# Recording the modulation's steps by the vector engine's spare time, and the norms' reciprocal roots in PSUM, in a two-block transformer kernel

## The chip, the cores and the metric

The kernel runs on one core of one Trainium2 chip. The metric is device microseconds (us) of one execution; a kernel's time is the median of its runs. The engines are named as in the profile: PE (TensorE, matrix multiplication), PEld (its weight loads), DVE (VectorE), ACT (ScalarE), POOL (GpSimd) and SP (SyncE, which issues the DMAs here).

## The reference, cut to what matters

Two stacks follow each other on one sequence of 512 tokens of width 1024. Each has two layers. All of it is float32.

```python
def first_block(x, c, w_mod, b_mod, ...):
    c_act = silu(c)
    for l in range(2):
        mod = (c_act @ w_mod[l] + b_mod[l]).reshape(1, 9, 1024)
        h = rmsnorm(x, g) * (1 + mod[:, 1]) + mod[:, 0]
        x = x + 0.5 * mod[:, 2] * swiglu(h, ...)
        h = rmsnorm(x, g) * (1 + mod[:, 4]) + mod[:, 3]
        x = x + mod[:, 5] * hybrid_mixer(h, ...)     # windowed attention, linear recurrence, short convolution
        h = rmsnorm(x, g) * (1 + mod[:, 7]) + mod[:, 6]
        x = x + 0.5 * mod[:, 8] * swiglu(h, ...)
    return rmsnorm(x, g_final)

def second_block(x, c, ctx, c_ctx, ...):             # 256 context tokens run beside the 512
    for i in range(2):
        m, mc = six vectors of silu(c) @ ada_w[i] + ada_b[i], and of c_ctx
        y, yc = mla_mixer(...) if i == 0 else na_mixer(...)
        h = layer_norm(ALPHA * h + g1 * y)
        h = layer_norm(ALPHA * h + g2 * conv_ffn(h * (1 + sc2) + sh2))
        # in layer 0 the same for the context
```

The modulation is the matrix-vector products `c_act @ w_mod` and `silu(c) @ ada_w`: 30 chunks of 1024 outputs that need only `c`, not `x`.

## The kernel before

Every activation stands transposed: eight tiles of 128 features by 512 tokens. A float32 operand is split into a rounded high part and a low part (`wh`, `wl` for weights, `hh`, `hl` and others for activations), and each product is three matmuls (`mm3`). So PE does three passes; ACT makes the high parts, DVE subtracts to get the low parts (`wl<-wr,wh`), and SP streams the weights, 256 KB a DMA.

The program is not issued as it is written. A `Recorder` collects all operations, `schedule` simulates them with a table of costs, and `emit` issues them in the order that this gave, one fixed queue for each engine. An operation's rank is its place in the recording. So where a step is *recorded* decides where the planner tries to place it, and each engine then runs its queue in order: an operation that isn't ready holds all behind it. The profile shows nearly every instruction at line 444, the issuing line in `emit`, so it is read by tile names.

`Core.run` draws the recording from three generators. `main` is the large chain. `side` is the context stream (tiles `hc`, `a`, matmuls `ps<-a,wh` of 256 columns), which gets a share of PE's recorded time and can't begin before the context's modulation of layer 0 is there (`ctx_stream` yields "wait" until then). The third is `gen_mods`, the modulation. One of its steps is one block of 128 outputs: two DMAs of 256 KB (`mr<-in_wmod`, `mr<-in_wada`), and for each a product with `silu(c)` with a row sum. Two of three products are one DVE instruction (`mr,c<-mr,b_c`, or `mj,c<-mr,b_c`); every third is a POOL product (`mr<-mr,b_c`) and an ACT sum. A step of `ada_w` that serves the context too has twice the products. DVE does 400 of these instructions in all, POOL 208. In the kernel before, `run` records one step for each 6150 ns of recorded PE time of `main`, evenly, whatever DVE has to do there; `mod` records the missing steps at once where a modulation is needed.

The stages by the trace, in us: start and first FFN of layer 0 to 405, its mixer to 605, second FFN to 1005, layer 1 the same (mixer 1430 to 1620) to 2095, latent attention to 2440, convolution FFN to 2860, neighbourhood attention to 3245, convolution FFN to the end.

A norm goes in three moves. `colsum` squares and adds the tiles and sums over features by matmuls with a column of ones (`ps<-ones,acc`) into a PSUM bank, one column for each 128 tokens. `rsqrt` makes the reciprocal root on DVE from an integer seed and three Newton steps of three instructions, on tiles of 128x2 or 128x4, each needing the one before. `bcast` transposes the result across the partitions (`ps<-ident,c`). There are 27 such roots: 3 over 512 tokens, 24 over 256. The norm of a stage is made by halves of 256 tokens (`rms_part`, `final_part`, `ln_part`), so that one half's norm can lie beside the other half's matmuls. In `ln_part` (layer norms) three of the eight subtractions `x<-x,bm` are DVE's and five are POOL's.

The planner knows that DVE and POOL hinder each other: `schedule` marks POOL's operations, and those of DVE that read and write no PSUM (`o.port`), and lets them wait for each other.

Of the kernel before, what the change touches and what calls it, by code (L numbers as in the profile page):

```python
# [16 lines left out]
ALU = mybir.AluOpType  # L17
AX = mybir.AxisListType

P = 128  # L20
D = 1024
KD = D // P
S = 512
C = 256
# [3 lines left out]
ALPHA = (2.0 * DEPTH) ** 0.25  # L28
# [32 lines left out]
LAGS = 2  # L61
FIRST = (100, 16)
HEAVY = 0.5
FIRST_POOL = (1, 3)
ON_DVE, ON_DVE_LAST = 1, 1
BEGIN = 20000.0
# [380 lines left out]
class Lag:  # L447
# [14 lines left out]
    def next(self):  # L462
        steps = self.q.pop(0)()
        if steps is not None:
            yield from steps
        yield


class Core:
# [171 lines left out]
    def first_mods(self):  # L641
# [3 lines left out]
        for m in range(8):  # L645
            nc.later = FIRST[0] + FIRST[1] * m
            dots = []
            for ch in range(2):
                d = [self.col(1), self.col(1)]
                for h in range(2):  # L650
                    raw = self.t(s="mr")
                    nc.sync.dma_start(raw, self.io["wmod"][0, ch * 8 + m][:, h * 512:(h + 1) * 512])
                    if (2 * ch + h) % 4 in FIRST_POOL:
                        nc.gpsimd.tensor_tensor(raw, raw, self.cb["c", h], op=ALU.mult)
# [67 lines left out]
        eng.tensor_tensor(acc, sums[0], sums[1], op=ALU.add)  # L722
        return acc

    def colsum(self, tiles, T, eng=None):
        nc = self.nc
        acc = self.total(tiles, T, eng)
        st = self.ps()
        for j in range(T // P):
            nc.tensor.matmul(st[:, j:j + 1], acc[:, j * P:(j + 1) * P], self.ones, start=True, stop=True)  # L730
        return st[:, :T // P]

    def rsqrt(self, v, n):
        nc = self.nc
        y, q = self.col(n), self.col(n)
        nc.vector.tensor_scalar(y.bitcast(I32), v.bitcast(I32), -0.5, float(0x5F3759DF), op0=ALU.mult, op1=ALU.add)
        for _ in range(3):
            nc.vector.tensor_tensor(q, y, y, op=ALU.mult)
            nc.vector.scalar_tensor_tensor(q, q, -0.5, v, op0=ALU.mult, op1=ALU.mult)
            nc.vector.scalar_tensor_tensor(y, q, 1.5, y, op0=ALU.add, op1=ALU.mult)  # L740
        return y

    def bcast(self, col, T, copy=None):
# [12 lines left out]
    def rms(self, x, T, width, eps=1e-6):  # L756
        nc = self.nc
        sq = []
        for a in x:
            q = self.t(s="sq")[:, :T]  # L760
            nc.scalar.activation(q, a, AF.Square)
            sq.append(q)
        st = self.colsum(sq, T)
        v = self.col(T // P)
        nc.vector.tensor_scalar(v, st, 1.0 / width, eps, op0=ALU.mult, op1=ALU.add)
        return self.bcast(self.rsqrt(v, T // P), T)

    def modulated(self, x, bc, G, Sh, out, T):
        nc = self.nc
# [100 lines left out]
    def run(self, main, side):  # L870


        rec = self.nc
        mods, own = BEGIN, 0.0
        due = 0.0
        mark = rec.pe
        for _ in main:
            own += rec.pe - mark
            due += self.share * (rec.pe - mark)
            while mods + self.every <= own:  # L880
                mods += self.every
                next(self.modgen, None)
            while side is not None and due > 0:
                mark = rec.pe + HEAVY * rec.ve
                got = next(side, "end")
                due -= rec.pe + HEAVY * rec.ve - mark
                if got == "end":
                    side = None
                elif got == "wait":
                    due = 0.0  # L890
            mark = rec.pe

    def rms_part(self, l, sub):

# [313 lines left out]
    def ln_part(self, xs, T, l, which, kind, mod, perm=False):  # L1208

        nc = self.nc  # L1210
        n = C // P
# [5 lines left out]
        def part(sl):  # L1217
# [8 lines left out]
            sq = []  # L1226
            for a in x:
                q = self.t(s="sq")[:, :C]
                nc.scalar.activation(q, a, AF.Square)
                sq.append(q)  # L1230
            s1 = self.colsum(x, C, nc.gpsimd)
            s2 = self.colsum(sq, C)
            mu, m2, v = self.col(n), self.col(n), self.col(n)
            nc.vector.tensor_scalar(mu, s1, 1.0 / D, None, op0=ALU.mult)
            nc.vector.tensor_tensor(m2, mu, mu, op=ALU.mult)
            bm = self.bcast(mu, C, self.t(s="bm"))
            nc.vector.tensor_scalar(v, s2, 1.0 / D, 1e-5 / (ALPHA * ALPHA), op0=ALU.mult, op1=ALU.add)
            nc.vector.tensor_tensor(v, v, m2, op=ALU.subtract)
            br = self.bcast(self.rsqrt(v, n), C)
            if T == C:  # L1240
                yield
            ts = []
# [596 lines left out]
```

## Time and profile before

| | us |
|---|---|
| median of 3 runs | 3613.79 (3612.24 to 3618.5) |
| the profiled execution, whole | 3614.32 |
| its span, first to last instruction | 3612.2 |
| PE busy in the span | 3482.7 |
| DVE busy | 2697.6 |
| ACT busy | 1815.6 |
| POOL busy | 772.5 |
| DMA, mean | 132 GB/s |

The whole execution is 2.1 us longer than the span. PE is busy in nearly all of it, so what can be won are the stretches in which PE waits, and those at its lower clock. "PEclk" in a row is the granted clock as a share of the upper level of 2.4 GHz; the records show that level and half of it, 1.2 GHz.

### The profile page before, as it was taken

Reading aid. Unit: us, or ns where it says so; the run is one execution under the profiler, and the core shown is the slowest. Engines: PE = TensorE matmul, PEld = TensorE weight load, DVE = VectorE, ACT = ScalarE, POOL = GpSimd, SP = SyncE. Lnnn points to the kernel's source line nnn. Section 1 sums busy time; section 2 is a strip of 40 time slices with the busy share of each in tenths; the row PEclk is TensorE's granted clock in tenths of the full one; section 3 lists DMA queues with packets and bytes.
Section 4 is the critical chain, followed back from the end, with each engine's and each line's share of the span. In section 5 each row is a group of like instructions: output and inputs, shape, how many; then the busy total and the mean of one; then the engine's idle time right before and its main releaser. Section 6 shows DMA issues by size and latency. Waiting matters only on the chain.

```text
span 3612.2 us, 56937 instructions
## 1 busy us (share of the span) xinstructions
PE 3482.7 (96%) x19814; PEld 3055.6 (85%) x19814; DVE 2697.6 (75%) x5566; ACT 1815.6 (50%) x3932; POOL 772.5 (21%) x848
## 2 busy tenths in 40 slices
PE   6999999999999999999999999989999999989998
PEld 5888978888898889899888988879888888978887
DVE  8966899986598866976444689988667757886566
ACT  5434565564456534844333578776334444454333
POOL 4311242331023410310000034341000422330002
PEclk9999999999999999999999999999999999999999
DMA  9854355675366564534334311214333143333330
GB/s 329 293 183 149 96 156 158 196 251 156 108 213 193 157 192 139 165 101 125 111 115 135 106 49 51 63 45 138 100 104 104 55 114 107 88 97 110 97 91 24
DMA packets 276448, 475.37 MB, mean 132 GB/s; under 512 B 40000, under 2 KB 55872, under 8 KB 276160
## 3 DMA queue, kind: packets, MB, share of 16 engines
q1 hardware_dynamic: 276160, 471.74, 43.0%
q8 instruction: 156, 2.56, 0.3%
q14 instruction: 132, 1.08, 0.1%
HBM read 448.81 MB, written 5.50 MB: 126 GB/s over the span
## 4 chain that ended last, share of the span: by engine, by line
PE 82%; DVE 11%; ACT 3%; issue 2%; DMA 1%; POOL 1%; SPq 0%; DVEq 0%; POOLq 0%; ACTq 0%
PE ps L444 82%; DVE c L444 2%; DVE wl L444 1%; DVE ptl L444 1%; DVE x L444 1%; DVE pl L444 1%; DVE mr L444 1%; DVE hl L444 1%; DVE tm L444 1%; DVE acc L444 0%; ACT L444 0%; DVE os L444 0%; DVE yl L444 0%; DVE mods L444 0%; DMA mr<-in_wada 0%
## 5 line engine op out<-in xcount | busy, mean ns | idle before, releaser
L444 DVE TENSOR_TENSOR wl<-wr,wh 128x512 fp32r<-128x512 f32 (+1 forms) x1182 | 835.1, 728 | 138.0 <-ACT wh L444 116.1
L444 ACT CAST wh<-wr 128x512 fp32r<-128x512 f32 (+1 forms) x1182 | 677.5, 614 | 112.2 <-PE ps L444 75.0
L444 PE MATMUL ps<-hh,wh 128*128 128x512 f32 (+1 forms) x1864 | 689.1, 370 | 4.4 <-ACT hh L444 4.4
L444 PE MATMUL ps<-hl,wh 128*128 128x512 f32 (+1 forms) x1864 | 686.7, 368 | 6.0 <-DVE hl L444 6.0
L444 PE MATMUL ps<-hh,wl 128*128 128x512 f32 (+1 forms) x1864 | 685.7, 368 | 2.1 <-DVE wl L444 1.9
L444 PE MATMUL ps<-fh,wh 128*128 128x512 f32 (+1 forms) x1344 | 463.6, 345 | 0.0
L444 PE MATMUL ps<-fl,wh 128*128 128x512 f32 (+1 forms) x1344 | 461.9, 344 | 0.0
L444 PE MATMUL ps<-fh,wl 128*128 128x512 f32 (+1 forms) x1344 | 461.7, 344 | 0.0
L444 PEld LDWEIGHTS ps<-hl,wh 128*128 128x128 f32 x1864 | 353.6, 190 | 63.6 <-DVE hl L444 8.4
L444 PEld LDWEIGHTS ps<-hh,wh 128*128 128x128 f32 x1864 | 353.7, 190 | 61.5 <-ACT hh L444 5.6
L444 PEld LDWEIGHTS ps<-hh,wl 128*128 128x128 f32 x1864 | 353.3, 190 | 60.5 <-DVE wl L444 2.9
L444 DVE SCALAR_TENSOR_TENSOR x<-ps,mods,x 128x512 f32<-128x512 f32 (+1 forms) x400 | 254.7, 640 | 199.3 <-PE ps L444 197.9
L444 PE MATMUL ps<-ah,wh 128*128 128x512 f32 (+1 forms) x1000 | 367.3, 367 | 6.4 <-ACT ah L444 6.4
L444 PE MATMUL ps<-al,wh 128*128 128x512 f32 (+1 forms) x1000 | 366.0, 366 | 0.5 <-DVE al L444 0.4
L444 PE MATMUL ps<-ah,wl 128*128 128x512 f32 (+1 forms) x1000 | 365.4, 365 | 0.0
L444 POOL TENSOR_TENSOR mr<-mr,b_c 128x512 f32<-128x512 f32 x123 | 185.9, 1514 | 473.8 <-DMA mr<-in_wmod 165.5
L444 PEld LDWEIGHTS ps<-fh,wl 128*128 128x128 f32 x1344 | 254.6, 189 | 30.0
L444 PEld LDWEIGHTS ps<-fh,wh 128*128 128x128 f32 x1344 | 254.6, 189 | 29.7
L444 PEld LDWEIGHTS ps<-fl,wh 128*128 128x128 f32 x1344 | 254.7, 190 | 29.5
L444 DVE SCALAR_TENSOR_TENSOR cv<-ps,ffc,cv 128x511 f32<-128x511 f32 (+1 forms) x264 | 173.2, 658 | 137.5 <-ACT cv L444 134.3
L444 ACT ACTIVATE cv<-ps,ffc 128x512 f32<-128x512 f32 (+1 forms) x132 | 93.4, 708 | 312.3 <-PE ps L444 311.9
L444 ACT CAST fh<-s 128x512 fp32r<-128x512 f32 x132 | 82.0, 621 | 295.7 <-DVE s L444 295.7
(328 smaller groups left out, 7008.1 us busy)
## 6 DMA issues: line engine op xcount, KB each, us to landing
wr<-in_gu SPq DMA_DIRECT2D x352, 256.0 KB, 3.1
mr<-in_wmod SPq DMA_DIRECT2D x288, 256.0 KB, 4.2
wr<-in_fin SPq DMA_DIRECT2D x264, 256.0 KB, 2.7
mr<-in_wada SPq DMA_DIRECT2D x192, 256.0 KB, 3.6
wr<-in_dn SPq DMA_DIRECT2D x176, 256.0 KB, 3.1
wr<-in_fout SPq DMA_DIRECT2D x132, 256.0 KB, 2.7
wr<-in_win SPq DMA_DIRECT2D x64, 256.0 KB, 3.0
wr<-in_nqkv SPq DMA_DIRECT2D x48, 256.0 KB, 3.1
```

The source lines that it names most:

```text
L444: getattr(eng, method)(*a, **k)
```

## The change

There are two edits. The first is in `run`. The fixed interval is gone. A balance `spare` grows with 0.7 of PE's recorded time and falls with DVE's recorded time, the side stream's included; it never falls below -5000 ns, and it starts at -20000 ns. After each piece of `main` and `side`, steps of the modulation are recorded as long as the balance is positive; each takes 500 ns and its own DVE time from it. The constant is `FILL, DEBT, STEP = 0.7, 5000.0, 500.0`.

The second is in the norms. `colsum` can give out two more columns groups of the same PSUM bank. `rsqrt` now keeps the variance `v` and the intermediate `q` there; only `y` is an SBUF column, so each of its instructions has a PSUM operand. The Newton step is written as `q = v*y`, `q = -0.5*q*y`, `y = (q+1.5)*y`, the width is folded into the last step's constants, and in `ln_part` one small instruction is saved.

```diff
-    def colsum(self, tiles, T, eng=None):
+    def colsum(self, tiles, T, eng=None, more=0):
...
-        return st[:, :T // P]
-
-    def rsqrt(self, v, n):
-        nc = self.nc
-        y, q = self.col(n), self.col(n)
+        n = T // P
+        return st[:, :n] if not more else tuple(st[:, i * n:(i + 1) * n] for i in range(more + 1))
+
+    def rsqrt(self, v, width, q):
+
+
+        nc = self.nc
+        y = self.col(v.width())
+        r = math.sqrt(width)
         nc.vector.tensor_scalar(y.bitcast(I32), v.bitcast(I32), -0.5, float(0x5F3759DF), op0=ALU.mult, op1=ALU.add)
-        for _ in range(3):
-            nc.vector.tensor_tensor(q, y, y, op=ALU.mult)
-            nc.vector.scalar_tensor_tensor(q, q, -0.5, v, op0=ALU.mult, op1=ALU.mult)
-            nc.vector.scalar_tensor_tensor(y, q, 1.5, y, op0=ALU.add, op1=ALU.mult)
+        for f in (1.0, 1.0, r):
+            nc.vector.tensor_tensor(q, v, y, op=ALU.mult)
+            nc.vector.scalar_tensor_tensor(q, q, -0.5 * f, y, op0=ALU.mult, op1=ALU.mult)
+            nc.vector.scalar_tensor_tensor(y, q, 1.5 * f, y, op0=ALU.add, op1=ALU.mult)
         return y
...
-        st = self.colsum(sq, T)
-        v = self.col(T // P)
-        nc.vector.tensor_scalar(v, st, 1.0 / width, eps, op0=ALU.mult, op1=ALU.add)
-        return self.bcast(self.rsqrt(v, T // P), T)
+        st, v, q = self.colsum(sq, T, more=2)
+        nc.vector.tensor_scalar(v, st, eps * width, None, op0=ALU.add)
+        return self.bcast(self.rsqrt(v, width, q), T)
...
-        mods, own = BEGIN, 0.0
-        due = 0.0
-        mark = rec.pe
+        spare, due = -BEGIN, 0.0
+        pe, ve = rec.pe, rec.ve
         for _ in main:
-            own += rec.pe - mark
-            due += self.share * (rec.pe - mark)
-            while mods + self.every <= own:
-                mods += self.every
-                next(self.modgen, None)
+            due += self.share * (rec.pe - pe)
...
-            mark = rec.pe
+            spare = max(spare + FILL * (rec.pe - pe) - (rec.ve - ve), -DEBT)
+            pe, ve = rec.pe, rec.ve
+            while spare > 0 and next(self.modgen, "end") != "end":
+                spare -= STEP + rec.ve - ve
+                ve = rec.ve
...
-            s2 = self.colsum(sq, C)
-            mu, m2, v = self.col(n), self.col(n), self.col(n)
+            s2, v, q = self.colsum(sq, C, more=2)
+            mu, m2 = self.col(n), self.col(n)
             nc.vector.tensor_scalar(mu, s1, 1.0 / D, None, op0=ALU.mult)
-            nc.vector.tensor_tensor(m2, mu, mu, op=ALU.mult)
+            nc.vector.scalar_tensor_tensor(m2, s1, -1.0, mu, op0=ALU.mult, op1=ALU.mult)
             bm = self.bcast(mu, C, self.t(s="bm"))
-            nc.vector.tensor_scalar(v, s2, 1.0 / D, 1e-5 / (ALPHA * ALPHA), op0=ALU.mult, op1=ALU.add)
-            nc.vector.tensor_tensor(v, v, m2, op=ALU.subtract)
-            br = self.bcast(self.rsqrt(v, n), C)
+            nc.vector.scalar_tensor_tensor(v, s2, 1e-5 * D / (ALPHA * ALPHA), m2, op0=ALU.add, op1=ALU.add)
+            br = self.bcast(self.rsqrt(v, D, q), C)
```

What this does to the queues, at three places. First DVE's queue at the very start, from the variance of the first norm on (`c`: small SBUF columns, `ps_155`: the bank of the sums, `mr`: a block of the modulation's weights, `b_c`: silu(c)). Before:

```order
L444 TENSOR_SCALAR c_163<-ps_155 128x4
L444 SCALAR_TENSOR_TENSOR mr_146,c_165<-mr_146,b_c_131 128x512
L444 TENSOR_SCALAR c_169<-c_163 128x4
L444 SCALAR_TENSOR_TENSOR mr_153,c_174<-mr_153,b_c_131 128x512
L444 SCALAR_TENSOR_TENSOR mods<-c_165,c_178,bmod 128x1
L444 SCALAR_TENSOR_TENSOR mods<-c_174,c_189,bmod 128x1
L444 SCALAR_TENSOR_TENSOR mods<-mods,gnorm 128x1
L444 TENSOR_TENSOR c_211<-c_169 128x4
L444 SCALAR_TENSOR_TENSOR mr_167,c_213<-mr_167,b_c_131 128x512
```

After, the same place:

```order
L445 TENSOR_SCALAR ps_155<-ps_155 128x4
L445 SCALAR_TENSOR_TENSOR mr_146,c_164<-mr_146,b_c_131 128x512
L445 TENSOR_SCALAR c_168<-ps_155 128x4
L445 TENSOR_TENSOR ps_155<-ps_155,c_168 128x4
L445 SCALAR_TENSOR_TENSOR ps_155<-ps_155,c_168 128x4
L445 SCALAR_TENSOR_TENSOR c_168<-ps_155,c_168 128x4
L445 SCALAR_TENSOR_TENSOR mr_153,c_176<-mr_153,b_c_131 128x512
L445 TENSOR_TENSOR ps_155<-ps_155,c_168 128x4
L445 SCALAR_TENSOR_TENSOR ps_155<-ps_155,c_168 128x4
L445 SCALAR_TENSOR_TENSOR c_168<-ps_155,c_168 128x4
```

The root's chain has moved ahead of modulation work: from the variance to the root's last instruction there are two products and one other instruction between its links, where there were six products and six others.

Second, DVE's queue where the context stream begins (`tm<-hc` and `a<-tm` make its first operand, `yl` and `x` are the mixer's last work). Before, in the mixer of layer 0:

```order
L444 SCALAR_TENSOR_TENSOR mj_5746,c_5747<-mr_5525,b_c_251_418 128x512
L444 TENSOR_TENSOR yl_5645<-ps_5724,yh_5626 64x128 x2
L444 SCALAR_TENSOR_TENSOR mj_5763,c_5764<-mr_5633,b_c_252_431 128x512
L444 SCALAR_TENSOR_TENSOR x_111<-ps_5710,mods,x_111 128x512
L444 SCALAR_TENSOR_TENSOR mr_5633,c_5781<-mr_5633,b_cc_478 128x512
L444 TENSOR_SCALAR tm_5786<-hc_4951,cm_86,cm_85 128x256
L444 TENSOR_SCALAR tm_5790<-hc_4951,cm_86,cm_85 128x256
L444 TENSOR_SCALAR tm_5794<-hc_4968,cm_86,cm_85 128x256
```

After, in the FFN behind it (`wl`, `s` and `fl` are that FFN's):

```order
L445 TENSOR_TENSOR wl_6516<-wr_6071,wh_6506 128x512
L445 TENSOR_SCALAR tm_6524<-hc_5723,cm_86,cm_85 128x256
L445 TENSOR_SCALAR tm_6530<-hc_5731,cm_86,cm_85 128x256
L445 TENSOR_SCALAR tm_6537<-hc_5731,cm_86,cm_85 128x256
L445 TENSOR_TENSOR wl_6542<-wr_6091,wh_6526 128x512
L445 TENSOR_SCALAR tm_6550<-hc_5760,cm_86,cm_85 128x256
L445 TENSOR_SCALAR tm_6557<-hc_5760,cm_86,cm_85 128x256
L445 SCALAR_TENSOR_TENSOR mr_5969,c_6362<-mr_5969,b_cc_496 128x512
```

The context stream begins later, since the chunks it waits for are recorded later, and its first matmul stands among the FFN's instead of among the mixer's output projection.

Third, DVE's queue at the last norm (`bm`: the broadcast mean). Before, from the second Newton step on:

```order
L444 TENSOR_TENSOR c_39678<-c_39676 128x2
L444 SCALAR_TENSOR_TENSOR c_39678<-c_39678,c_39670 128x2
L444 SCALAR_TENSOR_TENSOR c_39676<-c_39678,c_39676 128x2
L444 TENSOR_TENSOR x_98<-x_98,bm_39674 128x256
L444 TENSOR_TENSOR c_39678<-c_39676 128x2
L444 TENSOR_TENSOR x_107<-x_107,bm_39674 128x256
L444 SCALAR_TENSOR_TENSOR c_39678<-c_39678,c_39670 128x2
L444 TENSOR_TENSOR x_119<-x_119,bm_39674 128x256
L444 SCALAR_TENSOR_TENSOR c_39676<-c_39678,c_39676 128x2
```

After, from the first Newton step on:

```order
L445 TENSOR_TENSOR ps_39600<-ps_39600,c_39611 128x2
L445 SCALAR_TENSOR_TENSOR ps_39600<-ps_39600,c_39611 128x2
L445 TENSOR_TENSOR x_98<-x_98,bm_39613 128x256
L445 SCALAR_TENSOR_TENSOR c_39611<-ps_39600,c_39611 128x2
L445 TENSOR_TENSOR ps_39600<-ps_39600,c_39611 128x2
L445 TENSOR_TENSOR x_107<-x_107,bm_39613 128x256
L445 SCALAR_TENSOR_TENSOR ps_39600<-ps_39600,c_39611 128x2
L445 SCALAR_TENSOR_TENSOR c_39611<-ps_39600,c_39611 128x2
L445 TENSOR_TENSOR x_119<-x_119,bm_39613 128x256
```

The three subtractions stay inside the chain, and the first of them has moved forward, from the third Newton step into the first.

Counted over DVE's queue, the modulation's 400 products lie thus, before and after: 131 and 136 ahead of the first convolution of layer 0's mixer (`xc<-ps`), 25 and 9 from there to that mixer's last attention output (`yl<-ps,yh`, 64x128), 229 and 188 from there to layer 1's mixer, 15 and 6 in that mixer, 0 and 61 behind it.

## Rows read from the trace of the kernel before

**Rows 1.** The page, part 1: busy time, share of the span, instructions.

```profile
PE 3482.7 (96%) x19814; PEld 3055.6 (85%) x19814; DVE 2697.6 (75%) x5566; ACT 1815.6 (50%) x3932; POOL 772.5 (21%) x848
```

**Rows 2.** Stretches: length, busy us (instructions) per engine, PEclk, DMA share, GB/s.

```profile
core 0: us, PE busy (x) PEld busy (x) DVE busy (x) ACT busy (x) POOL busy (x), PEclk, DMA share, GB/s
0.00:40.00 40.00, 8.97 (x26) 6.40 (x26) 30.26 (x54) 25.66 (x52) 19.79 (x19) 1.00 0.99 355
90.00:180.00 90.00, 90.00 (x399) 74.53 (x398) 83.47 (x161) 39.31 (x92) 32.05 (x21) 1.00 0.89 294
180.00:270.00 90.00, 90.00 (x399) 74.53 (x398) 58.87 (x116) 29.60 (x64) 15.38 (x11) 1.00 0.60 186
400.00:620.00 220.00, 204.94 (x1312) 184.35 (x1311) 207.15 (x504) 135.66 (x338) 74.78 (x67) 0.97 0.48 147
1425.00:1620.00 195.00, 190.25 (x1231) 172.53 (x1230) 164.72 (x381) 119.29 (x285) 46.63 (x47) 0.99 0.49 149
...
2095.00:2440.00 345.00, 322.36 (x2105) 288.08 (x2106) 316.79 (x756) 277.50 (x673) 129.64 (x188) 0.97 0.18 51
```

**Rows 3.** PE's waits over the whole span: us in total, times, longest.

```profile
PE ps L444 <- DVE c L444: 25.5, 5, 13.5
```

**Rows 4.** PE's waits from 400 to 620 us.

```profile
PE ps L444 <- DVE wl L444: 4.4, 1, 4.4
PE ps L444 <- POOL P L444: 3.7, 2, 2.8
...
PE ps L444 <- ACT a L444: 0.9, 1, 0.9
```

**Rows 5.** Stretches, instructions that write or read `mr` alone.

```profile
core 0: us, DVE busy (x) ACT busy (x) POOL busy (x), PEclk, DMA share, GB/s
...
180.00:270.00 90.00, 19.28 (x54) 7.18 (x20) 15.38 (x11) 1.00 0.60 186
400.00:620.00 220.00, 50.84 (x126) 10.88 (x30) 45.10 (x31) 0.97 0.48 147
1425.00:1620.00 195.00, 19.44 (x44) 8.57 (x24) 17.65 (x11) 0.99 0.49 149
```

**Rows 6.** Groups of DVE by shape: busy, mean ns | idle before.

```profile
L444 DVE SCALAR_TENSOR_TENSOR mr<-mr,b_c 128x512 f32<-128x512 f32 x229 | 178.7, 795 | 0.3 <-DMA mr<-in_wada 0.2
...
L444 DVE DVE_READ_ACCUMULATOR mr<-mr,b_c 128x1 f32 x229 | 18.1, 79 | 0.0
```

**Rows 7.** Order of time, DVE at the start: start, us, what.

```profile
13.62 0.16 DVE L444 TENSOR_SCALAR c<-ps 128x4 f32<-128x4 f32 x1 [1.96 <-PE ps L444]
13.72 1.07 DVE L444 SCALAR_TENSOR_TENSOR mr<-mr,b_c 128x512 f32<-128x512 f32 x1
...
14.72 1.22 DVE L444 TENSOR_SCALAR c<-c 128x4 int32<-128x4 int32 x1
...
16.46 2.43 DVE L444 SCALAR_TENSOR_TENSOR mods<-c,c,bmod 128x1 f32<-128x1 f32 x2
...
25.70 1.21 DVE L444 SCALAR_TENSOR_TENSOR c<-c,c 128x4 f32<-128x4 f32 x1
```

**Rows 8.** Order of time, POOL at the start.

```profile
12.98 7.12 POOL L444 TENSOR_TENSOR mr<-mr,b_c 128x512 f32<-128x512 f32 x5 [11.67 <-DMA mr<-in_wmod]
```

**Rows 9.** Order of time, PE at the end of the start.

```profile
73.97 0.50 PE L444 MATMUL ps<-hl,wh 128*128 128x512 f32 x1 [0.56 <-DVE hl L444]
```

**Rows 10.** Order of time, DVE at the latent attention's last layer norm.

```profile
2425.67 0.16 DVE L444 TENSOR_SCALAR c<-ps 128x2 f32<-128x2 f32 x1 [0.43 <-PE ps L444]
2425.87 0.16 DVE L444 TENSOR_TENSOR c<-c,c 128x2 f32<-128x2 f32 x1
...
2426.42 0.98 DVE L444 TENSOR_TENSOR x<-x,bm 128x256 f32<-128x256 f32 x1
```

**Rows 11.** Order of time, DVE at the last layer norm.

```profile
3599.45 1.35 DVE L444 SCALAR_TENSOR_TENSOR c<-c,c 128x2 f32<-128x2 f32 x2
```

**Rows 12.** Order of time, POOL at the last layer norm.

```profile
3599.38 3.44 POOL L444 TENSOR_TENSOR x<-x,bm 128x256 f32<-128x256 f32 x5 [1.87 <-ACT bm L444]
```

**Rows 13.** PE's waits for `c` from 0 to 40, 2095 to 2440, 3520 to 3613 us.

```profile
PE ps L444 <- DVE c L444: 13.5, 1, 13.5
...
PE ps L444 <- DVE c L444: 5.5, 1, 5.5
...
PE ps L444 <- DVE c L444: 5.3, 1, 5.3
```

More of the change, by code (lines that the diff above doesn't have):

```diff
@@ L63 @@
 HEAVY = 0.5
+FILL, DEBT, STEP = 0.7, 5000.0, 500.0
 FIRST_POOL = (1, 3)
```

## The prediction

> **What bounds the kernel now.** I read the page's busy times first: PE works 3482.7 of 3612.2 us [rows 1]. What can be won is 129.5 us of idle PE, and what PE loses at its lower clock. So the next view is the table of stretches [rows 2], to see where PE's column falls short of the length. In the FFN (90 to 180, 180 to 270) PE is busy 90.00 of 90; whatever else happens there costs nothing. Short of its length it is in the first 40 us (8.97 busy), around layer 0's mixer (204.94 of 220, 15.1 idle), a little in layer 1's mixer (190.25 of 195, 4.8 idle) and in the latent attention (322.36 of 345, 22.6 idle). The DVE column shows why the first mixer is worse than the second, though both compute the same: DVE is busy 207.15 of 220 there (94%), and 164.72 of 195 (84%) in the second. The PEclk column adds to it: 0.97 of 220 is 6.6 us of clock lost, 0.99 of 195 is 2.0. Third, PE's waits over the span: the largest one is for `c`, the small columns of the norms: 25.5 us in five waits [rows 3]. Each edit goes at one of these two, so I cost them one by one.
>
> **The modulation's steps, in the two mixers.** PE's waits around the first mixer are for DVE's low parts (`wl`, 4.4), for POOL's scaling of the softmax (`P`, 3.7), and for the first operand of the context stream (`a`, 0.9) [rows 4]; the 4.4 and the 0.9 are one place, the context stream's first matmuls, which stand in PE's queue while DVE is behind. The modulation's share of that DVE time is 50.84 us in 400 to 620, and 45.10 us of POOL's; around the second mixer it is 19.44 and 17.65 [rows 5]. By the order, DVE's products between the first convolution and the last attention output fall from 25 to 9 in the first mixer and from 15 to 6 in the second. One product costs 795 ns and 79 ns to read its sum [rows 6], so 16 of them are 16 x 0.874 = 14.0 us less on an engine that has 12.85 us to spare in 220. That makes the first mixer, after, about what the second one is before: 4.8 idle and 2.0 of clock. The difference of the two, (15.1 - 4.8) + (6.6 - 2.0) = 14.9 us, is the upper bound. Below, it could be the 3.7 us behind POOL's `P` alone. The context stream's beginning moves to the FFN behind the mixer; by the order its operands are made some 45 us of matmul work before its first matmul, where before they were made in the same few us. So I count its 5.3 us as gone and nothing new for it. But the FFN's start carries it, the root of the second half and the first products together, so I take 12 and not 14.9. In the second mixer 9 products fewer are 7.9 us of DVE where it has 30 to spare and PE waits 4.8: between 0 and 4, I take 2.
>
> **Where the steps go.** They cost what they cost only where DVE is full. The 61 products now behind the second mixer stand in an FFN, like the rest. The densest place by the order is the first FFN: the matmuls of 180 to 270 now have about 50 products beside them where 27 were (54 instructions with their sums, [rows 5]). 23 more are 23 x 0.874 = 20.1 us, and DVE's 58.87 become 79 of 90 [rows 2]. The row of 90 to 180 has 83.47 with PE at 90.00, so the cover holds, and I cost it at nothing. Each product also brings a DMA of 256 KB past SP; those 90 us ran at 186 GB/s, and the row above them at 294 without a wait, so that is covered too. Without that cover each product would cost its 0.874 us.
>
> **The roots' instructions.** A link of the chain that reads PSUM took 0.16 while POOL was at work (13.62, inside POOL's 12.98 to 20.10) [rows 7, 8]; a link between SBUF columns took 1.22 (14.72) and 1.21 (25.70), one of four such in that chain, because it waits for POOL's instruction to end. In the layer norms the same links took 0.65 (1.35 for two) beside POOL's five subtractions, and 0.16 without them [rows 10 to 12]. In the changed kernel each link has a PSUM operand. No row shows a link that also writes PSUM; the nearest is the one that reads it, 0.16, and 0.2 from start to start [rows 10]. I take that; twice that, 0.4, is the other end.
>
> The rows show one price for PSUM and SBUF, 0.16 for each [rows 10]. The Trainium skill (Perfetto Trace Analysis, "Optimizing Scalar/DVE Operations") states against this change about 60 ns of access overhead for DVE on SBUF and about 125 on PSUM. By it each of 11 links would take 65 ns more, 0.7 us a chain, and with three exposed chains an estimate of 2 us less gained, 3594 in place of the time below. The row of 0.16 is a measured duration, and I go by it.
>
> *At the start* PE waits 13.5 us for this root [rows 13]. By the order only two products and one other instruction stand inside it now. From the variance: 0.2, the first product 1.1 (13.72) [rows 7], four links 0.8, the second product behind POOL's instruction about 1.1, four links 0.8, one blocked column 1.2 (half of 2.43) [rows 7], two links 0.4: 5.6 in place of 13.5, 7.9 sooner. That isn't yet won, since DVE is full from there to the last normalised tile, for which PE waits 0.56 at 73.97 [rows 9], and it has the same instructions left to do. What DVE is really spared is four links x (1.21 - 0.16) = 4.2, and some idle. I take 4.5; the ends are 1 and 8.
>
> *The two late layer norms* hold PE 5.5 and 5.3 us [rows 13]. Eleven links x 0.2 would be 2.2 us, 3.2 less each. But three subtractions stay inside the chain, both of their inputs in SBUF, and one that met POOL took 0.98 [rows 10]; 3 x 0.98 + 2.2 = 5.1 is 0.3 less. Between 0.3 and 3.2 I take 1 each. The other 22 roots lie beside matmuls; their shorter links and the boundary waits they feed (the other two waits for `c` are 25.5 - 13.5 - 5.5 - 5.3 = 1.2) I put at 1 together. That is 3, with ends 1 and 8.
>
> **Sum.** 12 + 2 + 4.5 + 3 = 21.5 us. The profiled execution took 3614.3, so 3592.8; it lies 0.5 above the median, so the forecast is 3592. The latent attention stays outside the sum: the context stream reaches it with some 15 us of matmul work more to do, which spills into the FFN behind; of its 22.6 idle us that can move 6 either way.
>
> **The rivals.**
> - *The mixer is not held by DVE.* PE's queue order, POOL's `P` and the shuffling DMAs hold it, and thinning the products only moves the wait. For it: PE waits 3.7 there for POOL. Against it: the twin stage with fewer products waits a third as much. Then only the context's place and the roots pay: 3614.3 - 8 = 3606.
> - *More is won.* Fewer waits also mean less time at the lower clock; if the mixer's whole 14.9, the start's 8 and 3.2 at both layer norms come, with 5 for the second mixer and the boundaries, it is 34: 3580.
> - *Slower: DVE fills up in the FFNs.* The place is the first FFN and the one behind the second mixer, where the products went. It decides from the point at which DVE passes 90 of 90: that is 11 us over the 79 reckoned above, or if a product beside POOL costs 1.35 in place of 0.874. Then a weight block's `wl` comes late with each product. If half of the 84 products that are new in these two places (23 and 61) held PE for 0.874, it would be 37 us: 3614.3 - 21.5 + 37 = 3630. Against it stands the row of 90 to 180, as dense and without a wait.
> - *The change doesn't do what it says.* Were steps missing where a modulation is due, `mod` would record them in a heap at a norm. By the order no heap is there. Time: 3614.
>
> **How the numbers follow.** The forecast has a chance of 0.66 (own range 3583 to 3602, from the mixer's 4 to 15, the start's 1 to 8 and the context's 6 either way), more won 0.13, the mixer not held by DVE 0.14, slower 0.05, no effect 0.02. The range of 8 in 10 is 3574 to 3609: it reaches into both neighbours. A measurement of this kernel can tell about 0.2% from no change, 7.2 us. Faster than 3606.6 are the forecast, more won and half of the mixer rival: 0.85; within 7.2 us 0.10; slower 0.05.
>
> **What would show it.** Right: around 400 to 620 PE's idle time falls to 5 to 8 us, no wait for `a` and none of 4.4 for `wl` at the context's begin; DVE there near 85%. The links `c<-ps,c` and `ps<-ps,c` take 0.16 to 0.2 beside POOL; the first wait for `c` falls from 13.5 to 6, and the first FFN's last `hl` comes 4 to 5 us sooner; the late waits for `c` are 2 to 5. Wrong: links of 0.4 or more, PE under 90.00 in the FFNs from 100 to 300 or behind the second mixer with `wl` as the releaser, or new waits in the latent attention larger than before.

## Result and profile after

The changed kernel takes 3569.19 us (median of 4 runs, 3566.67 to 3569.64); the kernel before, on the same chip, 3615.33. The ratio is 0.9871, with a 95% interval of 0.9854 to 0.9888. So it is 46 us faster, where 21.5 was forecast, and 5 us below the range's lower end. The profiled execution's span is 3564.9, 47.3 less than before.

The page's busy times after, which answer to [rows 1]:

```profile
PE 3465.7 (97%) x19814; PEld 3043.5 (85%) x19814; DVE 2671.6 (75%) x5556; ACT 1814.7 (51%) x3933; POOL 781.6 (22%) x848
```

PE has the same 19814 matmuls and is busy 17.0 us less. That is clock: the mean granted clock went from 0.988 to 0.994 of the upper level. The other 30 us are idle time.

The table of stretches after. The last two are shifted to the same work as before (25 and 23 us earlier); the columns are those of [rows 2]:

```profile
core 0: us, PE busy (x) PEld busy (x) DVE busy (x) ACT busy (x) POOL busy (x), PEclk, DMA share, GB/s
0.00:40.00 40.00, 13.60 (x41) 9.33 (x41) 30.74 (x62) 26.18 (x53) 19.42 (x19) 1.00 0.99 354
90.00:180.00 90.00, 90.00 (x399) 74.54 (x398) 84.28 (x163) 37.32 (x87) 31.81 (x22) 1.00 0.90 295
180.00:270.00 90.00, 90.00 (x399) 74.55 (x398) 81.54 (x163) 40.21 (x93) 34.85 (x22) 1.00 0.75 237
400.00:620.00 220.00, 214.41 (x1360) 192.73 (x1360) 192.59 (x464) 134.12 (x321) 53.88 (x54) 1.00 0.45 133
1400.00:1595.00 195.00, 191.24 (x1256) 174.36 (x1256) 171.93 (x399) 132.45 (x308) 45.04 (x48) 1.00 0.43 127
2072.00:2417.00 345.00, 326.31 (x2223) 295.54 (x2221) 318.98 (x751) 269.30 (x658) 136.62 (x197) 0.99 0.20 59
```

Around the first mixer PE's idle time is 5.6 us, where it was 15.1, and the clock is at the upper level throughout; in the FFN PE is still at 90.00 of 90, though DVE has gone from 58.87 to 81.54 in 180 to 270. The instructions on `mr` alone, as in [rows 5], say why:

```profile
180.00:270.00 90.00, 37.52 (x98) 11.55 (x32) 34.85 (x22) 1.00 0.75 237
400.00:620.00 220.00, 29.05 (x71) 6.51 (x18) 27.37 (x18) 1.00 0.45 133
```

PE's waits over the whole span, which answer to [rows 3] (total, times, longest):

```profile
PE ps L445 <- DVE acc L445: 14.3, 4, 11.8
PE ps L445 <- DVE wl L445: 11.8, 7, 3.8
PE ps L445 <- DVE c L445: 10.3, 6, 4.5
PE ps L445 <- DVE ptl L445: 9.1, 17, 1.9
PE ps L445 <- DVE yl L445: 6.4, 2, 6.1
```

The wait for `c` has gone from 25.5 to 10.3. DVE at the start, in order of time, against [rows 7]:

```profile
13.67 0.17 DVE L445 TENSOR_SCALAR ps<-ps 128x4 f32<-128x4 f32 x1 [1.96 <-PE ps L445]
13.75 1.18 DVE L445 SCALAR_TENSOR_TENSOR mr<-mr,b_c 128x512 f32<-128x512 f32 x1
...
14.87 0.15 DVE L445 TENSOR_SCALAR c<-ps 128x4 int32<-128x4 int32 x1
15.05 0.17 DVE L445 TENSOR_TENSOR ps<-ps,c 128x4 f32<-128x4 f32 x1
...
17.86 0.16 DVE L445 SCALAR_TENSOR_TENSOR c<-ps,c 128x4 f32<-128x4 f32 x1
```

POOL's products run here as before, from 13.12 on:

```profile
13.12 7.06 POOL L445 TENSOR_TENSOR mr<-mr,b_c 128x512 f32<-128x512 f32 x5 [11.81 <-DMA mr<-in_wmod]
```

But the links (the instructions of the root's chain) take 0.15 to 0.17 and start 0.2 apart. The root ends at 18.0, 4.3 after the variance.

**Where the 47 us went.** To compare equal work, I took for each matmul the time to the start of the next, less the median of that for its shape (227 ns for 512 columns, 120 for 256, 109 for a transpose). Summed, this is what PE loses by waits and clock together. The table is worked out from the traces, one profiled execution of each kernel; the stretches hold equal matmul work, and are named by times of the kernel before. "Steps only" and "roots only" are the first two experiments. Executions of one kernel lie up to 12 us apart (`steps_only`), so a us or two in a single line says little.

| place | before | after | steps only | roots only | gain | forecast |
|---|---|---|---|---|---|---|
| start, first FFN (to 389) | 39.4 | 35.6 | 39.0 | 34.5 | 3.8 | 4.5 |
| mixer of layer 0 (442 to 664) | 21.6 | 8.3 | 11.4 | 21.5 | 13.3 | 12 |
| mixer of layer 1 (1472 to 1599) | 7.7 | 4.1 | 2.2 | 7.7 | 3.6 | 2 |
| latent attention (2079 to 2471) | 41.5 | 33.1 | 35.4 | 37.7 | 8.4 | 1 |
| conv FFN into neighbourhood attention (2772 to 2996) | 23.3 | 18.0 | 21.9 | 17.3 | 5.3 | } |
| all other places, mostly the ends of stages | 53.9 | 40.7 | 50.5 | 41.7 | 13.2 | } 2 |

The mixers and the start came out about as large as forecast. The two lines at the bottom, 18.5 us where 2 were forecast, and the latent attention are the error.

### The profile page after: what moved, and what is told of

It is laid out like the page before. It is cut to its first block, busy times and chain, and to the rows that moved or that the text cites. A ratio compares the mean times of both kernels' runs of the same rounds, so it can differ in the third digit from the quotient of the medians.

```text
span 3564.9 us, 56991 instructions
## 1 busy us (share of the span) xinstructions
PE 3465.7 (97%) x19814; PEld 3043.5 (85%) x19814; DVE 2671.6 (75%) x5556; ACT 1814.7 (51%) x3933; POOL 781.6 (22%) x848
## 5 line engine op out<-in xcount | busy, mean ns | idle before, releaser
L445 DVE TENSOR_TENSOR wl<-wr,wh 128x512 fp32r<-128x512 f32 x1182 | 846.4, 736 | 124.5 <-ACT wh L445 96.5
L445 ACT CAST wh<-wr 128x512 fp32r<-128x512 f32 x1182 | 677.8, 613 | 111.7 <-PE ps L445 64.4
```

What stands on the lines that cost most here:

```text
L445: getattr(eng, method)(*a, **k)
```

## Experiments

The kernel before was run beside each group and had medians of 3612 to 3615; the ratios are against those runs. The changed kernel was not run again, so differences to its 3569.19 are between groups.

**One edit alone.** `steps_only` has the new `run` and the old roots; `roots_only` the old `run` and the new roots (the diffs are the two halves of the one above).

> Only the first edit: the modulation's steps recorded by DVE's spare time, the roots in SBUF columns as before. Theory A (the stages' gains belong to the edit that was meant for them: the steps win the two mixers, the roots win the start, the late norms and the latent attention): the first mixer's 15 us and the second's 3 come, the start's 4 and the 24 behind the second mixer don't: 3597. Theory B (the latent attention's 12 us come from the context stream, which the steps make later, so that its matmuls still stand there while the layer norm runs): the 12 come as well: 3585. If the two edits only work together: 3605 or more.

Measured: 3591.05, ratio 0.9929 (0.9916 to 0.9943), 24 us less than before.

> Only the second edit: the roots in PSUM, the modulation's steps every 6150 ns as before. Theory A: the start's 4 us, the latent attention's 12 and some 12 at the other norms come, the mixers' 18 don't: 3588. Theory B: the latent attention's 12 don't come: 3600. Theory of the prediction (8 us for all roots): 3607.

Measured: 3587.71, ratio 0.9923 (0.9909 to 0.9936), 27 us less. So the two edits are worth about the same, and sum to 51, of which 46 are left when both are made: at the end of the first FFN, for instance, each alone wins the same 2 us. By the table the roots win 18 of their 27 us at the ends of stages, 5 at the start and 4 in the latent attention; the steps win 16 in the mixers, 6 in the latent attention and 5 elsewhere (27 in the profiled execution, which was 3 faster against the kernel before than the median). Theory A hit the roots' number; the steps' lies halfway between A and B.

**The links, with the order held.** Operand names apart, every queue of this kernel is that of the changed kernel; only the place of `v` and `q` differs. `also` tells the planner, and it alone, that the bank is written.

```diff
-        y = self.col(v.width())
+        y, z = self.col(v.width()), self.col(v.width())
...
-            nc.vector.tensor_tensor(q, v, y, op=ALU.mult)
+            nc.vector.tensor_tensor(z, v, y, op=ALU.mult, also=(q,))
...
         st, v, q = self.colsum(sq, T, more=2)
+        v = self.col(T // P)
...
```

> The changed kernel with every engine's order kept as it is, but v and q of all 27 roots are SBUF columns, so that each link again has all its operands in SBUF. Theory of the links (each link beside POOL costs 0.65 to 1.2 in place of 0.16): the start gives back 4 to 5 us and the late norms 1 to 3 each: 3577 to 3583. Theory of the order (what the second edit wins is that the planner no longer keeps the root's links back while POOL is at work; how long a link takes is a small matter): within 3 us of the changed kernel, 3569 to 3572.

Measured: 3589.16, ratio 0.9925 (0.9912 to 0.9937), 20 us more than the changed kernel. The links' theory holds, and with more than its own number, which was 8 to 14. Since both kernels have the same order, the 297 links (11 for each of 27 roots) can be set side by side one by one. 227 of them meet no POOL instruction in the kernel with columns: 161 ns with `v` and `q` in PSUM, 158 with both in SBUF. 70 do: 157 ns and 632. That is 33 us of links. It is not all lost: the rest of DVE's instructions take 10 us less with the columns, 3.7 of it the 24 subtractions `x<-x,bm` (569 ns each, 724 in the changed kernel). By these lengths, a part of the contention had only moved from the links to other instructions with SBUF operands. DVE as a whole is busy 22.3 us more, and the kernel is 20 us longer.

How they reach it is seen best where the convolution FFN ends. DVE with the roots in SBUF columns, in order of time:

```profile
2834.03 0.16 DVE L445 SCALAR_TENSOR_TENSOR c<-ps,c 128x2 f32<-128x2 f32 x1 [0.29 <-PE ps L445]
...
2834.31 0.74 DVE L445 TENSOR_SCALAR c<-c 128x2 int32<-128x2 int32 x1
2834.96 0.41 DVE L445 TENSOR_TENSOR x<-x,bm 128x256 f32<-128x256 f32 x1
2835.30 0.68 DVE L445 TENSOR_TENSOR c<-c,c 128x2 f32<-128x2 f32 x1
...
2836.91 0.68 DVE L445 SCALAR_TENSOR_TENSOR c<-c,c 128x2 f32<-128x2 f32 x1
...
2838.19 0.68 DVE L445 TENSOR_TENSOR wl<-wr,wh 128x512 fp32r<-128x512 f32 x1
```

The same instructions in the changed kernel:

```profile
2821.16 0.17 DVE L445 SCALAR_TENSOR_TENSOR ps<-ps,c 128x2 f32<-128x2 f32 x1 [0.29 <-PE ps L445]
...
2821.43 0.15 DVE L445 TENSOR_SCALAR c<-ps 128x2 int32<-128x2 int32 x1
2821.50 0.94 DVE L445 TENSOR_TENSOR x<-x,bm 128x256 f32<-128x256 f32 x1
2822.36 0.15 DVE L445 TENSOR_TENSOR ps<-ps,c 128x2 f32<-128x2 f32 x1
...
2823.22 0.15 DVE L445 SCALAR_TENSOR_TENSOR c<-ps,c 128x2 f32<-128x2 f32 x1
...
2823.69 0.74 DVE L445 TENSOR_TENSOR wl<-wr,wh 128x512 fp32r<-128x512 f32 x1
```

From the variance to the first low part `wl` it is 4.2 us in the one, 2.5 in the other. PE does not wait for a norm there; it waits for that `wl`, 5.3 and 3.4 us:

```profile
PE ps L445 <- DVE wl L445: 5.3, 1, 5.3
```

```profile
PE ps L445 <- DVE wl L445: 3.4, 1, 3.4
```

(The waits of the two stretches, 2780 to 2910 and 2770 to 2895.) So a slow link is charged to whatever stands behind it in DVE's queue, under that tile's name. The Trainium skill (SBUF — State Buffer, "Who interferes with whom") says that a DVE instruction with at most one SBUF input, outside the modes that take both ports, doesn't contend with GpSimd, and that one with two contends with a GpSimd instruction that reads SBUF. The 157 and 632 ns agree. The Trainium skill (Perfetto Trace Analysis, "Optimizing Scalar/DVE Operations") has the overheads from which the prediction made its estimate of 65 ns more for a link in PSUM. The measured durations don't show it: the 227 undisturbed pairs differ by 3.

**The context's place in the latent attention.** Three kernels move the context stream alone. The first is the kernel before, with the stream held until the second FFN:

```diff
-        while ("ax", 0, 2) not in self.mcol:
+        while ("ax", 0, 2) not in self.mcol or not self.past:
             yield "wait"
...
-        yield from self.ffn(x, h2, f"gu2_{l}", f"dn2_{l}", ("w", l, 8), S, after=part)
+        for i, _ in enumerate(self.ffn(x, h2, f"gu2_{l}", f"dn2_{l}", ("w", l, 8), S, after=part)):
+            self.past = self.past or i == 6
+            yield
```

> The kernel before with one thing changed: the context stream may begin only in the second FFN of layer 0, so that its first matmul stands after 593 us of matmul work, as in the changed kernel, and not after 497. Steps and roots as before. Theory A (the first mixer is won by thinning the products, the context's place is worth the 5.3 us of the waits at its begin): 3610. Theory B (the context's place is what counts, in the first mixer and again in the latent attention): 15 + 12 us less, 3588. If only the latent attention follows it: 3598.

Measured: 3610.74, ratio 0.9984 (0.9975 to 0.9993). That is A's number, but by another way: by the table's measure the first mixer loses 24.7 us in place of 21.6, the latent attention 35.0 in place of 41.5. So the 5.3 us at the context's begin are not won by moving it: DVE is still full, and the wait moves. From 400 to 640 us PE's longest wait is now for the norm's sum:

```profile
PE ps L444 <- DVE acc L444: 7.8, 2, 7.4
```

(The profiled execution of this kernel took 3604.22, 6.5 us less than its median; the two places are read from that one.)

The other two are the changed kernel with another share of matmul time for the context:

```diff
-SHARE, SHARE_MLA, EVERY = 0.22, 0.2987, 6150
+SHARE, SHARE_MLA, EVERY = 0.235, 0.2987, 6150
```

> The changed kernel, but the context stream gets 0.235 of the recorded matmul time in place of 0.22. It still begins after 593 us of matmul work, and has caught up with the kernel before by the latent attention (1242 and 1248 of its matmuls issued at 2150 us of matmul work, where the changed kernel has 1104). Theory B (the later context is what wins 8.5 us in the latent attention): 3577, with the loss between 2060 and 2440 us. Theory A (those us have another cause): 3569.

Measured: 3577.18, ratio 0.9896 (0.9881 to 0.9911), 8.0 more than the changed kernel, as B said. The latent attention loses 42.9 in place of 33.1; the other places together don't change.

> The changed kernel, but the context stream gets 0.213 of the recorded matmul time in place of 0.22, so it is further behind in the latent attention (1082 matmuls at 2150 us of matmul work in place of 1104; its last one 27 us of work later). If the lag wins because context matmuls fill PE's waits at the layer norm, more lag wins no less: 3566 to 3569. If what counts is how the two streams happen to meet, it can go either way: 3564 to 3577.

Measured: 3582.19 (share 0.213), ratio 0.9911 (0.9897 to 0.9926), 13 more. The latent attention, at 41.8, is 8.7 of it; the rest is spread over other places, none above 3. So more lag is not better. The longest waits of the latent attention with no lag, with the change as it is, and with more lag:

```profile
PE ps L445 <- DVE ptl L445: 11.3, 7, 7.2
```

```profile
PE ps L445 <- DVE yl L445: 6.4, 2, 6.1
```

```profile
PE ps L445 <- DVE ptl L445: 8.3, 7, 6.2
PE ps L445 <- DVE c L445: 3.8, 1, 3.8
```

The layer norm's work lies in DVE's queue ahead of a low part of the softmax (`ptl`) or of the output (`yl`) that PE needs next, and which one, and with how much ready beside it, depends on where the context stands. So the context's place alone moves this stage by 9 to 10 us in the changed kernel. It isn't the only source of the 8.4 us won there: the roots alone, with the context where it was, win 3.8, the steps alone 6.1. Why this place is a good one is not settled.

**How much the mixer is held by DVE.** `steps_early` is the kernel before with steps every 4350 ns up to layer 0's mixer and none in it:

```diff
+        self.hold = False
...
+        self.hold = not l
         yield from self.mixer(l, x, h1, part)
+        self.hold, self.every = False, EVERY
...
-                next(self.modgen, None)
+                if not self.hold:
+                    next(self.modgen, None)
...
-        self.share, self.every = SHARE, EVERY
+        self.share, self.every = SHARE, 4350
```

> The kernel before, roots as before, with the steps every 4350 ns up to layer 0's mixer and none recorded while it is; from there on every 6150 ns. DVE has 6 products in that mixer in place of 25, and 152 ahead of it in place of 131; the context stream still begins at the mixer's end (after 526 us of matmul work, before 497). Theory of thinning (DVE's fullness holds the mixer, the context's place does not matter there): 400 to 620 us gives 12 to 14 us, and the latent attention, where the context is between the two kernels, 0 to 8: 3594 to 3603. Rival (the context's later begin and thinning are both needed in the mixer, since each alone leaves a full stretch): under 6 us in the mixer, 3608 or more.

Measured: 3588.49, ratio 0.9932 (0.992 to 0.9945). The stretch 400 to 620 in four kernels: context held, steps only, steps early, and the changed kernel without steps in the mixers:

```profile
400.00:620.00 220.00, 203.56 (x1271) 183.29 (x1270) 204.66 (x505) 134.28 (x330) 76.79 (x69) 0.95 0.47 148
```

```profile
400.00:620.00 220.00, 214.15 (x1358) 193.57 (x1357) 194.03 (x466) 133.47 (x320) 53.06 (x54) 0.98 0.43 130
```

```profile
400.00:620.00 220.00, 217.47 (x1464) 200.18 (x1464) 191.00 (x459) 137.57 (x331) 48.66 (x51) 1.00 0.43 135
```

```profile
400.00:620.00 220.00, 215.03 (x1353) 194.10 (x1352) 185.71 (x449) 131.31 (x314) 48.12 (x51) 0.98 0.41 126
```

With DVE at 204.66 or more PE has 203.56 or 204.94; with DVE at 194 or less it has 214 to 217. With 6 products and the context still beginning at the mixer's end the mixer loses 3.9 us in place of 21.6: thinning does it, and more than the 14.9 that the prediction had as its upper end, while moving the context alone won nothing in the mixer.

> The changed kernel, but no step of the modulation is recorded while a mixer is (9 and 6 products in the two mixers become 3 and none). If DVE's load still holds the mixers: 2 to 4 us less, 3566. If at 9 products the mixer is already held by its own chain: 3569. The context stream begins 32 us of matmul work later for it.

```diff
+        self.hold = False
...
+        self.hold = True
         yield from self.mixer(l, x, h1, part)
+        self.hold = False
...
-            while spare > 0 and next(self.modgen, "end") != "end":
+            while spare > 0 and not self.hold and next(self.modgen, "end") != "end":
```

Measured: 3576.01, ratio 0.9893 (0.9878 to 0.9907). The first mixer doesn't get better with 3 products for 9 (10.5 for 8.3), the second a little with none for 6 (2.3 for 4.1); so at 9 products their number no longer holds the first. What does isn't settled: with 6 products and an earlier context (`steps_early`) it lost only 3.9. The latent attention, with the context 32 us of work later, loses 43.0 in place of 33.1. Neither expectation had that.

**Where the FFN's cover ends.**

```diff
-FILL, DEBT, STEP = 0.7, 5000.0, 500.0
+FILL, DEBT, STEP = 0.9, 5000.0, 500.0
```

> The changed kernel with 0.9 in place of 0.7 as the share of matmul time that DVE may fill. 219 of the 400 products stand ahead of the first mixer in place of 136, and the context stream begins after 273 us of matmul work. Theory of the prediction's slower rival, past its point (83 more products of 0.874 us are 73 us on DVE, which had 68 of 325 to spare in the first FFN): low parts come late, PE falls below its length from 75 to 400 us, by 5 us or more, and the latent attention finds the context nearly done: 3585 to 3600. If the FFN's queues bear it all the same: PE at 325 of 325 there, and only the latent attention changes, 3569 to 3580.

Measured: 3632.33, ratio 1.0051 (1.0035 to 1.0066), some 19 us slower than the kernel before. The stretches 90 to 180 and 270 to 400, and PE's waits in the second:

```profile
90.00:180.00 90.00, 90.00 (x399) 74.51 (x397) 89.88 (x181) 43.86 (x104) 35.05 (x24) 1.00 0.91 314
270.00:400.00 130.00, 120.66 (x588) 101.06 (x587) 121.41 (x244) 64.21 (x151) 55.24 (x35) 0.99 0.63 196
```

```profile
PE ps L445 <- DVE wl L445: 9.3, 5, 3.9
```

This is the prediction's slower rival, past its point: from 270 to 400 every wait of PE is for `wl`, with DVE at 121.41 of 130. From the start to the mixer the kernel loses 43 us more than the changed one, which has 76.06 of 130 of DVE in this stretch and PE at 129.75. But the share of one stretch doesn't mark the point: from 90 to 180 DVE is at 89.88 of 90, and PE loses nothing.

**The subtractions in the root's chain.** In the layer norms DVE reads the mean from its PSUM bank; POOL keeps the copy.

```diff
-            bm = self.bcast(mu, C, self.t(s="bm"))
+            bp = self.bcast(mu, C)
+            bm = self.t(s="bm")[:, :C]
+            nc.scalar.copy(bm, bp)
...
-                (nc.vector if k % 3 < (ON_DVE if mod else ON_DVE_LAST) else nc.gpsimd).tensor_tensor(x[k], x[k], bm, op=ALU.subtract)
+                if k % 3 < (ON_DVE if mod else ON_DVE_LAST):
+                    nc.vector.tensor_tensor(x[k], x[k], bp, op=ALU.subtract)
+                else:
+                    nc.gpsimd.tensor_tensor(x[k], x[k], bm, op=ALU.subtract)
```

> The changed kernel, and DVE's subtractions of the mean in the layer norms (24 of 256 columns, 724 ns each) read the broadcast mean from its PSUM bank and not from the SBUF copy; POOL's five of eight keep the copy. Theory of the port (a DVE instruction with two SBUF operands waits for POOL's instruction, one with a PSUM operand does not): each falls to about 0.42, the length of other PSUM subtractions of that width, 24 x 0.3 = 7 us less of DVE, most of it ahead of an exposed norm: 3563 to 3566. If a chain of the norm is bound elsewhere: 3569.

Measured: 3562.27, ratio 0.9853 (0.9837 to 0.987), 6.9 us less than the changed kernel and the lowest median of all. The intervals of the two ratios overlap; but all eight runs of the two kernels that read the mean from PSUM (this one and the next, 3559.45 to 3565.74) lie below all four of the changed kernel (from 3566.67). The edit takes back, and more, what the change itself had cost these subtractions. The 24 subtractions by DVE in the kernel before, the changed kernel and this one (columns as in [rows 6]):

```profile
L444 DVE TENSOR_TENSOR x<-x,bm 128x256 f32<-128x256 f32 x24 | 11.8, 498 | 1.1 <-ACT bm L444 1.1
```

```profile
L445 DVE TENSOR_TENSOR x<-x,bm 128x256 f32<-128x256 f32 x24 | 17.4, 724 | 0.6 <-ACT bm L445 0.4
```

```profile
L445 DVE TENSOR_TENSOR x<-x,ps 128x256 f32<-128x256 f32 x24 | 9.8, 414 | 3.7 <-ACT bm L445 3.1 <-PE ps L445 0.6
```

With the links quick, the subtractions come to lie beside POOL's. In the last layer norm of the changed kernel a subtraction took up to 0.98:

```profile
3553.30 0.98 DVE L445 TENSOR_TENSOR x<-x,bm 128x256 f32<-128x256 f32 x1
...
3554.46 0.68 DVE L445 TENSOR_TENSOR x<-x,bm 128x256 f32<-128x256 f32 x1
```

and with the mean from PSUM 0.42:

```profile
3549.96 0.42 DVE L445 TENSOR_TENSOR x<-x,ps 128x256 f32<-128x256 f32 x1 [0.24 <-PE ps L445]
```

The last norm itself gains little by it: PE's wait for `c` there goes from 3.7 to 3.2. In the latent attention, which loses 30.9 for 33.1, the wait of 6.1 for `yl` is gone.

> The kernel with the mean read from PSUM, and in the last layer norm DVE takes six of the eight subtractions and POOL two, in place of three and five. If the five of POOL are what its last norm ends on (3.44 us for five of POOL's, 6 x 0.42 = 2.5 for DVE's six): 1 to 2 us less than that kernel, 3561. If DVE's root ends last: the same or up to 1 us more, 3562 to 3563.

```diff
-ON_DVE, ON_DVE_LAST = 1, 1
+ON_DVE, ON_DVE_LAST = 1, 2
```

Measured: 3563.19, ratio 0.9864 (0.985 to 0.9877): the same within what can be told apart. POOL's five are not what the last norm ends on.

> The steps as in the kernel with early steps (every 4350 ns up to layer 0's mixer, none in it), the roots in PSUM, and the mean of the layer norms read by DVE from PSUM. If the three gains add (23.7 + 27.3 + 6.9 less than 3612, less the 5 by which the two edits of the change together fall short of their sum): 3559. If the latent attention, with the context elsewhere once more, gives its 8 back: 3567.

The edits of `steps_early` and `mean_in_psum` on the changed kernel's roots. Measured: 3572.54, ratio 0.9891 (0.9875 to 0.9908). It is above both expectations; the gains don't add. Set against `mean_in_psum`, the first mixer loses only 4.1 (9.3 there), but the second, where steps are recorded evenly again and 23 products stand in place of 6, 14.1 in place of 4.2, and the latent attention 37.1 in place of 30.9.

## Why the prediction was wrong, step by step

- **The first mixer, 12 (4 to 14.9): right,** 13.3. The mechanism, DVE's products, is shown by `steps_early` and `context_held`. Only the upper end was too low, as the 17.7 of `steps_early` show: the twin stage was no floor. It was held by its own 15 products: it loses 7.7 with them, 4.1 with 6, and 10 to 14 with the 24 and 23 of `steps_early` and of the last experiment.
- **"I count its 5.3 us as gone"**, for the context's begin: right in the sum, wrong in the reason. Moved alone, the context takes its wait along.
- **The second mixer, 2: right** in kind, 3.6.
- **The FFN covers the steps: right.** 79 of 90 was reckoned, 81.54 measured, PE at 90.00. Its rival was right that `wl` comes late past some point; that the point is DVE's share of a stretch doesn't hold (89.88 of 90 without a loss in `fill_09`).
- **The links, 0.16 to 0.2: right,** 0.15 to 0.17 beside POOL. **The start, 4.5: right in size,** 3.8; the wait for `c` is 4.5 us there, where 6 was forecast. The path isn't shown: the last `hl`, which was to come 4 to 5 us sooner, ends at 72.94 where it ended at 73.91. Before and after:

```profile
73.17 0.74 DVE L444 SCALAR_TENSOR_TENSOR hl<-tm,mods,hh 128x512 fp32r<-128x512 f32 x1
```

```profile
71.29 1.65 DVE L445 SCALAR_TENSOR_TENSOR hl<-tm,mods,hh 128x512 fp32r<-128x512 f32 x1
```

- **The two late layer norms, 1 each: right in mechanism.** The three subtractions did stay in the chain, and at the last norm up to 0.98 long; the wait for `c` there is 3.7 in place of 5.3. In the latent attention the wait for `c` (5.5) is gone, but one of 6.1 for `yl` has come: a new wait larger than before, which the prediction had named as a sign against it, though the stage as a whole won 8.4.
- **"The other 22 roots lie beside matmuls ... I put at 1 together": this step failed.** By the kernel with the order held the links' length is worth 18 of 23 us (the difference of the two profiled executions) at the stages' ends, and by `roots_only` it is 18 of 27; about 2 of it is at the last norm. I took PE's waits named `c` for all that the roots cost [rows 3, 13], and those are the waits in which the root itself came last. The roots also lengthened DVE's queue at the stages' ends, and that stood under other names, as for the `wl` shown above where the convolution FFN ends; the other ends were not followed instruction by instruction. A view of before would have told it: DVE's groups by shape (columns as in [rows 6]), where the 144 links of two columns that end a Newton step or its product last 270 ns on average against the 160 of an undisturbed one, 16 us of DVE in this group alone (an upper bound, since a part of it moves to the next instruction):

```profile
L444 DVE SCALAR_TENSOR_TENSOR c<-c,c 128x2 f32<-128x2 f32 x144 | 38.4, 270 | 2.6
```

- **"The latent attention stays outside the sum ... 6 either way": this failed too.** The stage won 8.4 us, and with either of two other places of the context it would have won nothing (42.9 and 41.8 lost, 41.5 before). I named the resource that decides (where the context stands) and put its size too low.

The profiled executions lie 47.6 us apart by the table, 26 more than forecast (25 by the medians). Of these 26 the stages' ends account for 16.5, the latent attention for 7.4 and the mixers for 2.9; the start gave 0.7 less.

## What to carry to other kernels

Price a blocked instruction by its engine's whole queue, not by the waits that carry its name: take the groups by shape, set the mean against the shortest instance and multiply by the count. That is an upper bound, since contention that leaves one instruction can fall on the next: here the links' 33 us came to 22 of DVE and 20 of the kernel. Scratch of a chain of small DVE instructions belongs in a PSUM bank that is open anyway, if POOL works beside it; so do DVE's larger operands where they are in PSUM already. Spread optional work by what the engine has to spare, and leave a margin over the whole stage: with 0.7 of matmul time for DVE PE lost 0.25 us from 90 to 400, with 0.9 it lost 9.3 from 270 to 400. One stretch doesn't tell: with 0.9 DVE was at 89.88 of 90 from 90 to 180, and PE lost nothing there yet.

## What the runs showed of the hardware

A DVE instruction on two or four columns took 157 ns on average with a PSUM operand where POOL was at work, and 632 with its operands in SBUF, up to 1.25 us, near the 1.4 of one POOL product (7.06 us for five). PSUM cost nothing in exchange: 161 against 158 ns. A subtraction on 128x256 took 498 to 728 ns on average with both inputs in SBUF, up to 0.99 us, and 414 with one read from PSUM.

Less waiting did not always bring clock. The changed kernel has 30 us less idle time, and PE was busy 17 us less for the same matmuls, at a mean granted clock of 0.994 for 0.988. The roots alone took 28 us of idle time away, but the clock stayed at 0.988, and PE was busy 0.9 us more:

```profile
PE 3483.6 (97%) x19814; PEld 3057.7 (85%) x19814; DVE 2683.6 (75%) x5556; ACT 1815.0 (51%) x3932; POOL 780.0 (22%) x848
```

The steps alone took 8.0 us off PE's busy time, at 0.991. Which waits cost clock is not settled.
